# Low weight halves by negated copy and adding DMA in a mixer-and-retrieval block

## The chip, the cores and the metric

The kernel runs on one core of a Trainium2 chip. The metric is device time in microseconds for one execution; a lower time is better. The time before is the median of three runs; beside them one execution was recorded by the hardware profiler, and all durations below are from that one. PE is the matrix engine (TensorE), PEld its weight loads, DVE the VectorE, ACT the ScalarE, POOL the GpSimd, SP the SyncE, which here only issues DMAs.

## The reference

The block has a mixer (norm, modulation, one input projection, a gated short convolution beside a linear recurrence, one output projection) and a retrieval layer with 128 x 128 experts. The second is most of the work:

```python
q = (xb @ w_q).reshape(p, PEER_HEADS, 2, PEER_DK_HALF)
sc = jnp.einsum('phcd,hcnd->phcn', q, sub_keys)
top_s, top_i = lax.top_k(sc, PEER_TOPK)
...
best_s, best_pos = lax.top_k(cand_s, PEER_TOPK)
idx = jnp.take_along_axis(cand_i, best_pos, axis=-1)
g = jax.nn.softmax(best_s, axis=-1)
u_sel = expert_u[idx]
act = jax.nn.gelu(jnp.einsum('phkd,pd->phk', u_sel, xb), approximate=False)
coef = g * act
return jnp.einsum('phk,phkd->pd', coef, expert_v[idx])
```

There are 512 tokens of width 1024, 8 heads, and 16 of 16384 experts for each head and token. All is float32.

## The kernel before, in words

**Dense and sparse.** The 512 tokens are four tiles of 128. For 320 tokens (`NU`) the product with `expert_u` is dense: all 128 blocks of 128 experts ("u chunks") are multiplied on PE and go through Gelu. For the other 192, tile 0 and the first 64 tokens of tile 1 (`XB`), the chosen rows are gathered by indirect DMAs and multiplied on DVE, one row of 128 partitions at a time ("dots", `dots`, line 788): 64 for the part of tile 1 and 128 for tile 0. For tiles 1 to 3 the product with `expert_v` is dense as well ("v chunks"), with coefficients that are the Gelu times a gate matrix. Tile 0 takes 128 gathered sums instead (`sums`, line 804). Dots and sums are 320 steps, each a gather of 512 KB on POOL's queue and one DVE instruction.

**Split weights.** A float32 product is done in three matmuls of a rounded format (`mm3`, lines 92 to 94): high weight by high activation, high by low, low by high. Each weight block of 128 x 1024 is loaded by SP (`load_w`, ring `wraw` of `WR` = 4), rounded by ACT (`high`, line 78, ring `whi` of `WB` = 4), and its low half is the difference, made by DVE (`low`, line 83, ring `wlo` of 4). A buffer of a ring comes free when its last reader is done.

**The order.** After the mixer come the eight query blocks, one a head, and behind each the scores against the keys. The first selections (`stage1` for heads 0 to 3) lie beside them on DVE. Then a hand-written order begins. Iteration `k` of the u loop issues `weights(k)` (the load of block `k + 5`, the low half of block `k + 2`), the matmuls of u chunk `k` with the Gelu of the chunk before, then other work that a planner chooses, and at its end the high half of block `k + 3`. Every engine runs its own queue in the order issued.

**The planner.** It books planned nanoseconds for PE, DVE and ACT (`pe`, `dve`, `ac`), and takes pieces of four generators while `dve` is below `pe`: `s` the selections (top-16, softmax, indices) of tile 1 and then of 2, 3 and 0; `r` the remaining `stage1` pieces; `g` the gate matrices, made from one-hot rows on DVE, ACT and PE and stored to DRAM (`Gd`); `d` the dots. A u chunk books 3530 for PE, 1140 for DVE (the low half) and 1400 for ACT. Dots may start at iteration `first[0]`, four after tile 1's selection is done, and are taken while fewer than `DR * (k + 1 - first[0])` are given, until `CE - QU` = 118. Gates are spread evenly over the chunks from the point where `r` ends. Dots that are left at chunk 124 and all sums are spread evenly over the v chunks. There the gate matrices come back from `Gd`, mostly in reads for 16 chunks at a time (`load_g16`), and some activations from `Ad`.

Of the kernel before, what the change touches and what calls it, by code (L numbers as in the profile page):

```python
# [8 lines left out]
F32 = mybir.dt.float32  # L9
FR = mybir.dt.float32r  # L10
# [3 lines left out]
AF = mybir.ActivationFunctionType  # L14
OP = mybir.AluOpType
# [4 lines left out]
KB = 8  # L20
# [14 lines left out]
def block_kernel(ctx, tc, xT, small, w_ada1, w_ada, b_ada, w_in, w_r, w_i, w_out, w_q, keys, uT, u, v, final_g, out):  # L35
    nc = tc.nc
# [4 lines left out]
    wring = ctx.enter_context(tc.tile_pool(name="wring", bufs=2))  # L41
# [29 lines left out]
    def load_w(src):  # L71
        raw = wring.tile([128, KB, 128], F32, name="wraw", bufs=WR)
        nc.sync.dma_start(raw, src)
        return raw

    def high(raw):
        hi = wring.tile([128, KB, 128], FR, name="whi", bufs=WB)
        nc.scalar.activation(hi, raw, AF.Copy)  # L78
        return hi

    def low(raw, hi):
        lo = wring.tile([128, KB, 128], FR, name="wlo", bufs=WB)
        nc.vector.tensor_sub(lo, raw, hi.bitcast(F32))  # L83
        return lo

    def split_w(raw):
        hi = high(raw)
        return hi, low(raw, hi)

    def mm3(ps, hi, lo, xh, xl, ks, first, last):  # L90
        for k in ks:
            nc.tensor.matmul(ps, hi[:, k, :], xh(k), start=first and k == ks[0], stop=False)  # L92
            nc.tensor.matmul(ps, hi[:, k, :], xl(k), start=False, stop=False)  # L93
            nc.tensor.matmul(ps, lo[:, k, :], xh(k), start=False, stop=last and k == ks[-1])  # L94
# [140 lines left out]
    z_, tn, e_, w_, w2, ac = (l4[:, i, :] for i in range(6))  # L235
# [85 lines left out]
    for cb in range(4):  # L321
# [29 lines left out]
        h = mt("h")  # L351
# [32 lines left out]
    for m in range(KB):  # L384
        if m + 2 < KB:
            oraw[m + 2] = load_w(w_out[m + 2])
        hi, lo = split_w(oraw[m])
# [9 lines left out]
    def x1_mm(i):  # L397
        t, e = divmod(i, 2)
        pt = psZ.tile([128, 4, 128], F32, name="ps_z", bufs=3)
        for k in range(4):  # L400
            nc.tensor.transpose(pt[:, k, :], xs[:, 4 * e + k, t * 128:(t + 1) * 128], ident)
        return i, pt

    def x1_out(i, pt):
        t, e = divmod(i, 2)
        xn = qp.tile([128, T], F32, name="xn")
        nc.scalar.activation(xn, pt, AF.Copy)
        nc.gpsimd.dma_start(x1d[t * 128:(t + 1) * 128, e * 512:(e + 1) * 512], xn)  # L408
# [21 lines left out]
                nc.scalar.activation(dst[:, (k - 3) * 128:(k + 1) * 128], src, AF.Copy)  # L430

    tp_cur = []
    qraw = {0: load_w(w_q[0]), 1: load_w(w_q[1])}
    for k in range(KB):
        t1 = sq_pool.tile([128, T], F32, name="mt1")
        nc.vector.tensor_mul(t1, xs[:, k, :], psr2)
# [35 lines left out]
    qsp = {}  # L472
    early = chain(*(stage1([h], range(NT)) for h in range(HQ)))

    for h in range(8):
        if h + 2 < 8:
            qraw[h + 2] = load_w(w_q[h + 2])
        if h == 0:
            qsp[0] = split_w(qraw[0])
        if h + 1 < 8:  # L480
            qsp[h + 1] = split_w(qraw[h + 1])
        hi, lo = qsp[h]
        ps = psZ.tile([128, T], F32, name="ps_z", bufs=3)
        mm3(ps, hi, lo, lambda k: h2h[:, k, :], lambda k: h2l[:, k, :], range(KB), True, True)
        qT = qp.tile([128, T], F32, name="qT")
        nc.scalar.activation(qT, ps, AF.Copy)
        pss = [psZ.tile([128, NT, 128], F32, name="ps_g", bufs=2) for c in range(2)]
        for t in range(NT):
            for c in range(2):
                nc.tensor.matmul(pss[c][:, t, :], qT[64 * c:64 * c + 64, t * 128:(t + 1) * 128],  # L490
                                 keys_sb[64 * c:64 * c + 64, h, :], start=True, stop=True)
        for _ in range(6 if h >= 2 else 0):
            next(early, None)
        for c in range(2):
            sc[h, c] = scs.tile([128, NT, 128], F32, name="sc", bufs=SCB)
            nc.scalar.activation(sc[h, c], pss[c], AF.Copy)
        if h + 3 < 8:
            x1_out(*x1_mm(h + 3))
# [315 lines left out]
    jobs = [("u", c) for c in range(CE)]  # L814
# [4 lines left out]
    wraw, whi, wlo = {}, {}, {}  # L819
    v0 = max(CE - RB + 3, 0) // 8 * 8 + 8  # L820
    vorder = list(range(v0, NE)) + list(range(v0))
# [7 lines left out]
    def w_high(k):  # L829
        if k < len(jobs):  # L830
            whi[k] = high(wraw[k])

    def w_low(k):
        if k < len(jobs):
            wlo[k] = low(wraw.pop(k), whi[k])

    def weights(k):
        w_load(k + 5)
        w_low(k + 2)
# [4 lines left out]
    def spill(q):  # L844
        nc.sync.dma_start(Ad[q], act[q].rearrange("p c t -> p (c t)"))
        act[q] = None
# [3 lines left out]
    def u_evict():  # L850
        if unread:
            c, ps = unread.pop()
            if c % 2 == 0:
                act[c // 2] = ring.tile([128, 2, NU], F32, name="act", bufs=RB // 2)
            nc.scalar.activation(act[c // 2][:, c % 2], ps, AF.Gelu)  # L855

    def u_chunk(k, pool):
        c = jobs[k][1]
        ps = pool.tile([128, NU], F32, name="ps_act", bufs=2)
        mm3(ps, whi.pop(k), wlo.pop(k), hd, ld, range(KB), True, True)  # L860
        u_evict()
        unread.append((c, ps))
        q = c // 2 - RB // 2 + 2
        if c % 2 == 0 and 0 <= q < v0 // 2:
            spill(q)
        pe[0] += 3530
        dve[0] += 1140
        ac[0] += 1400

    gbuf, g16, gdone = {}, {}, set()  # L870
    coef = {}
# [34 lines left out]
    def v_act(q):  # L906
        if q < NE // 2:
            c = vorder[2 * q] // 2
            if act[c] is None:
                act[c] = ring.tile([128, 2, NU], F32, name="act", bufs=RB // 2)  # L910
                nc.sync.dma_start(act[c].rearrange("p c t -> p (c t)"), Ad[c])
# [24 lines left out]
    pe, dve, ac = [0], [-HEAD], [0]  # L936
# [6 lines left out]
    def turn(k):  # L943

        awake = [g for g in "gsrd" if g in gens and asleep[g] <= k]
        if "d" in awake and (given["d"] >= DR * (k + 1 - first[0]) or k >= CE - QU or xd > k % 2):
            awake.remove("d")
# [16 lines left out]
    for k in range(3):  # L964
        w_high(k)
    for k in range(2):
        w_low(k)
    manual = ExitStack()
    manual.enter_context(tc.manual_schedule())
    for k in range(CE):  # L970
        weights(k)
        u_chunk(k, psE)
        gates_low(4)
        cur[0] = k
# [8 lines left out]
        while dve[0] < RHO * pe[0] or k == KD:  # L983
# [18 lines left out]
            if gopen or g == "d":  # L1002
                given[g] += {"g": 0, "d": 1}.get(g, n)
        w_high(k + 3)
        if k == KD:
            ep.close()
# [47 lines left out]
    for k in range(CE, len(jobs)):  # L1054
        w_load(k + 5)
        w_high(k + 3)
        w_low(k + 2)
        kind, n = jobs[k]
        if kind == "u":
            u_chunk(k, psP)  # L1060
        else:
            q, e = divmod(n, 2)
            v_gates(n + 5)
            if e == 0:
                v_act(q + 4)
                v_gated(q + 1)
            else:
                v_rest(q + 1)
            vsp[n] = [w.pop(k).rearrange("p k e -> p (k e)") for w in (whi, wlo)] + [c[:, e] for c in coef[q]]
            if n < NE - VT:  # L1070
                for b in range(3):
                    v_chunk(n, b)
                del vsp[n]
            u_evict()
            pe[0] += 4090
            dve[0] += 2005
        if kind == "v":
            share = min(max(n + 1 - QV, 0) / (NE - VE - QV), 1) * (steps + 0.31 * (NE - RB)) - 0.31 * max(n + 1 - RB, 0)
            while done < share and next(sparse, None):
                done += 1  # L1080
# [53 lines left out]
XD = 2  # L1134
CE = 124
GB_E = 5
DR = 1.1
QU = 6
QV = 3
RB = 32  # L1140
ZL = 1
XE = 5
WB = 4
# [51 lines left out]
```

## Time and profile before

| | us |
|---|---|
| median of 3 runs | 1411.64 |
| lowest, highest | 1409.84, 1411.95 |
| the profiled execution | 1413.22 |
| its span | 1411.5 |

| stretch of the span, us | what runs |
|---|---|
| 0 to 255 | modulation, mixer, output projection, second norm |
| 255.0 to 309.3 | eight query blocks and scores |
| 309.3 to 403.7 | u chunks 0 to 23 |
| 403.7 to 832.1 | u chunks 24 to 123 |
| 832.1 to 863.2 | v chunks 0 to 3, u chunks 124 to 127 between them |
| 863.2 to 1382.8 | v chunks 4 to 124 |
| 1382.8 to 1411.5 | the last three v chunks, last additions, final norm |

The share of busy time on the page is an average over these stretches, and each has its own limit; busy time by stretch and the waits within one say more. Matmuls are pipelined: a PE that is busy all the time is at its peak only if the count of matmuls in the stretch is also at its highest. In the groups of instructions the columns are line, engine, operation, output from inputs, shapes, count, then busy time and mean nanoseconds, then the engine's idle time just before with what ended it.

### The profile page before, as it was taken

The page shows a single profiled execution, that of the slowest core. Times are in us where ns is not written, and L with a number is a line of the kernel's source. Part 1 is how long each engine was busy: PE and PEld are TensorE (multiplying, and loading weights), DVE is VectorE, ACT ScalarE, POOL GpSimd, SP SyncE. Part 2 cuts the span into 40 slices and gives each one's busy share as a digit, 9 for nine tenths or more (in the row PEclk, how much of TensorE's full clock was granted, in tenths as well). Part 3 has the DMA queues.
Part 4 walks back from the last instruction along what each step waited for, and adds up shares of the span by engine and source line. Part 5 has one row for each costly group of instructions (what it writes and reads, how often), then busy time and mean ns, then how long its engine had stood idle before and what let it go on. Part 6 is the DMA issues. An engine that isn't in the chain of part 4 may idle for free.

```text
span 1411.5 us, 21746 instructions
## 1 busy us (share of the span) xinstructions
PE 1336.9 (95%) x7739; PEld 1144.7 (81%) x7739; DVE 1222.1 (87%) x2332; ACT 687.6 (49%) x1178; POOL 538.0 (38%) x334
## 2 busy tenths in 40 slices
PE   5999998999998999999999999899989999999995
PEld 2666787779998999998989998777778888878884
DVE  6766555899998999999989847799989889898998
ACT  4544433545377697797744444233333434343442
POOL 0000000000233145344545404576666667576760
PEclk9999999999999999999999999999999999999998
DMA  9675322124678899999999997999999999999994
GB/s 378 225 265 181 124 90 97 61 83 134 203 253 300 290 344 397 357 355 355 417 382 388 403 314 244 411 378 410 403 415 411 404 404 416 412 405 410 406 382 165
DMA packets 146929, 440.07 MB, mean 312 GB/s; under 512 B 14722, under 2 KB 42370, under 8 KB 144772
## 3 DMA queue, kind: packets, MB, share of 16 engines
q1 hardware_dynamic: 99812, 267.75, 51.5%
q0 software_dynamic: 46720, 169.89, 30.8%
q8 instruction: 60, 0.98, 0.3%
q10 hardware_dynamic: 288, 1.05, 0.2%
q14 instruction: 49, 0.40, 0.1%
HBM read 393.54 MB, written 45.09 MB: 311 GB/s over the span
## 4 chain that ended last, share of the span: by engine, by line
DVE 27%; PE 23%; DMA 16%; issue 13%; ACT 4%; DVEq 0%; SPq 0%; ACTq 0%
DMA wraw<-in_v_dram 13%; DVE wlo L83 5%; PE ps_act L92 5%; PE ps_act L94 5%; PE ps_act L93 5%; PE acc L1037 5%; DVE scr L788 4%; DVE ys L804 4%; DMA Gd<-stg 2%; DVE cf L920 2%; DVE cl L931 2%; DVE oh L627 2%; ACT whi L78 1%; DVE rep L457 1%; PE ps_gt L658 1%
## 5 line engine op out<-in xcount | busy, mean ns | idle before, releaser
L78 ACT ACTIVATE whi<-wraw 128x1024 fp32r<-128x1024 f32 x292 | 308.7, 1057 | 404.1 <-DMA wraw<-in_v_dram 157.7
L83 DVE TENSOR_TENSOR wlo<-wraw,whi 128x1024 fp32r<-128x1024 f32 x292 | 356.1, 1220 | 112.5 <-ACT whi L78 111.3
L92 PE MATMUL ps_act<-h,whi 128*128 128x320 f32 x1024 | 322.5, 315 | 8.1 <-ACT act L855 6.9
L94 PE MATMUL ps_act<-h,wlo 128*128 128x320 f32 x1024 | 317.1, 310 | 0.6 <-DVE wlo L83 0.6
L93 PE MATMUL ps_act<-h,whi 128*128 128x320 f32 x1024 | 317.1, 310 | 0.0
L767 POOL DMA_INDIRECT rows<-in_u_dram,idx_s x128 | 201.3, 1573 | 189.0 <-DVE scr L788 162.4
L767 POOL DMA_INDIRECT rows<-in_v_dram,idx_s x128 | 222.7, 1740 | 108.7 <-DVE ys L804 84.9
L1037 PE MATMUL acc<-whi,ch 128*128 128x512 f32 x750 | 233.7, 393 | 9.5 <-ACT ch L924 9.2
L1037 PE MATMUL acc<-whi,cl 128*128 128x512 f32 x750 | 234.6, 394 | 6.1 <-DVE cl L931 6.1
L1037 PE MATMUL acc<-wlo,ch 128*128 128x512 f32 x750 | 233.6, 393 | 0.0
L767 POOL DMA_INDIRECT rows<-in_u_dram,idx_b x64 | 108.9, 1701 | 255.7 <-DVE scr L788 171.8
L92 PEld LDWEIGHTS ps_act<-h,whi 128*128 128x128 f32 x1024 | 193.2, 189 | 10.8 <-ACT act L855 8.7
L94 PEld LDWEIGHTS ps_act<-h,wlo 128*128 128x128 f32 x1024 | 192.9, 188 | 0.9 <-DVE wlo L83 0.9
L93 PEld LDWEIGHTS ps_act<-h,whi 128*128 128x128 f32 x1024 | 193.3, 189 | 0.2
L1037 PEld LDWEIGHTS acc<-whi,ch 128*128 128x128 f32 x750 | 141.6, 189 | 40.7 <-ACT ch L924 10.9
L1037 PEld LDWEIGHTS acc<-whi,cl 128*128 128x128 f32 x750 | 141.6, 190 | 40.1 <-DVE cl L931 11.1
L1037 PEld LDWEIGHTS acc<-wlo,ch 128*128 128x128 f32 x750 | 142.1, 189 | 29.9
L804 DVE SCALAR_TENSOR_TENSOR ys<-rows,acts,ys 128x1024 f32<-128x1024 f32 x127 | 162.6, 1281 | 1.7
L788 DVE SCALAR_TENSOR_TENSOR scr<-rows,h2n 128x1024 f16<-128x1024 f32 x128 | 156.2, 1220 | 2.3 <-DMA rows<-in_u_dram,idx_s 0.6
L643 ACT ACTIVATE igh<-oh,gl 128x128 f16<-128x128 f16 x320 | 104.0, 432 | 47.8 <-DVE oh L627 47.6
L408 POOL DMA_DIRECT2D x1d<-xn x8 | 4.6, 569 | 281.7 <-DVE wlo L83 234.6
L92 PE MATMUL ps_z<-h,whi 128*128 128x512 f32 x224 | 90.8, 409 | 3.2 <-ACT h L216 2.9
(260 smaller groups left out, 1691.2 us busy)
## 6 DMA issues: line engine op xcount, KB each, us to landing
wraw<-in_uT_dram SPq DMA_DIRECT2D x128, 512.0 KB, 6.8
wraw<-in_v_dram SPq DMA_DIRECT2D x128, 512.0 KB, 9.3
Gd<-stg SPq DMA_DIRECT2D x46, 512.0 KB, 9.2
wada<-in_w_ada_dram SPq DMA_DIRECT2D x16, 1024.0 KB, 5.1
Ad<-act SPq DMA_DIRECT2D x48, 320.0 KB, 7.1
act<-Ad SPq DMA_DIRECT2D x48, 320.0 KB, 12.2
h<-Gd SPq DMA_DIRECT2D x12, 1024.0 KB, 18.3
wraw<-in_w_in_dram SPq DMA_DIRECT2D x20, 512.0 KB, 6.1
```

Of the source, the lines that this page charges most:

```text
L78: nc.scalar.activation(hi, raw, AF.Copy)
L83: nc.vector.tensor_sub(lo, raw, hi.bitcast(F32))
L92: nc.tensor.matmul(ps, hi[:, k, :], xh(k), start=first and k == ks[0], stop=False)
L93: nc.tensor.matmul(ps, hi[:, k, :], xl(k), start=False, stop=False)
L94: nc.tensor.matmul(ps, lo[:, k, :], xh(k), start=False, stop=last and k == ks[-1])
L627: nc.vector.tensor_tensor(flat.rearrange("p (q n b) -> p q n b", q=8, b=2), io2[:, None, :, :].to_broadcast(shp), sij[:, a0].rearrange("p ...
L643: nc.scalar.activation(ig[:, 1, k // 2, :, k % 2], of[:, k // 2, 0, :, k % 2], AF.Copy, scale=gl[:, t0 + k:t0 + k + 1])
L767: nc.gpsimd.indirect_dma_start(out=r[:, :], out_offset=None, in_=table, in_offset=bass.IndirectOffsetOnAxis(ap=idxs[:, k:k + 1], axis=0))
L788: nc.vector.scalar_tensor_tensor(scr, rows.pop(n), 1.0, hn, op0=OP.mult, op1=OP.mult, accum_out=dst[:, k:k + 1])
L804: nc.vector.scalar_tensor_tensor(ys, rows.pop(k), acts[:, k:k + 1], ys, op0=OP.mult, op1=OP.add)
L920: nc.vector.tensor_mul(cf[:, :, XB:].rearrange("p c (g t) -> p c g t", t=16), act.pop(vorder[2 * q] // 2).rearrange("p c (g t) -> p c g t" ...
L1037: nc.tensor.matmul(accs[b][e], st[:, bs], mv[:, e * 512:(e + 1) * 512], start=first, stop=last)
```

## The change

The low half is raw minus high. The new helper forms it in another order: ACT writes the negated high half into the low buffer, and a DMA that adds to its destination brings the raw block from DRAM onto it. That DMA is issued from POOL's queue. The helper is used for u blocks 3 to 23 (21 of them) and query blocks 2 to 7 (six). The ACT copy and the POOL DMA of block `k + 3` stand at the end of iteration `k`, where only the high half stood; the DVE subtraction of these blocks, which stood at the start of iteration `k + 1`, is gone. The raw block is still loaded by SP for the high half, so it is read from DRAM twice. Query blocks are loaded one head earlier, and their high half is formed two heads ahead, not one. The planner books nothing on DVE for these low halves and 2350 instead of 1400 on ACT. `DR` goes from 1.1 to 1.2.

```diff
+    def low_dma(src, hi):
+        lo = wring.tile([128, KB, 128], FR, name="wlo", bufs=WB)
+        nc.scalar.activation(lo, hi.bitcast(F32), AF.Copy, scale=-1.0)
+        nc.gpsimd.dma_start(lo, src, accum_op=OP.add)
+        return lo
...
-    qraw = {0: load_w(w_q[0]), 1: load_w(w_q[1])}
+    qraw = {h: load_w(w_q[h]) for h in range(3)}
...
-        if h + 2 < 8:
-            qraw[h + 2] = load_w(w_q[h + 2])
+        if h + 3 < 8:
+            qraw[h + 3] = load_w(w_q[h + 3])
         if h == 0:
             qsp[0] = split_w(qraw[0])
-        if h + 1 < 8:
-            qsp[h + 1] = split_w(qraw[h + 1])
+            qsp[1] = split_w(qraw[1])
+        if h + 2 < 8:
+            whq = high(qraw[h + 2])
+            qsp[h + 2] = whq, low_dma(w_q[h + 2], whq)
...
     def w_high(k):
         if k < len(jobs):
             whi[k] = high(wraw[k])
+            if 3 <= k < LN:
+                del wraw[k]
+                wlo[k] = low_dma(uT[jobs[k][1]], whi[k])
 
     def w_low(k):
-        if k < len(jobs):
+        if k < len(jobs) and k not in wlo:
             wlo[k] = low(wraw.pop(k), whi[k])
...
-        dve[0] += 1140
-        ac[0] += 1400
+        dve[0] += 0 if 3 <= k + 2 < LN else 1140
+        ac[0] += 2350 if 3 <= k + 3 < LN else 1400
...
-DR = 1.1
+DR = 1.2
...
+LN = 24
```

## The prediction

> **What bounds the kernel now.** I read the page's busy shares first, then its chain that ended last, then busy time stage by stage, then the waits inside the stages.
>
> ```profile
> PE 1336.9 (95%) x7739; PEld 1144.7 (81%) x7739; DVE 1222.1 (87%) x2332; ACT 687.6 (49%) x1178; POOL 538.0 (38%) x334
> DVE 27%; PE 23%; DMA 16%; issue 13%; ACT 4%; DVEq 0%; SPq 0%; ACTq 0%
> ```
>
> PE looks full, but the chain changes hands between DVE, PE and DMA, so what an edit is worth has to be read stage by stage. The stage table has, for each stretch, its length, then busy time and count of PE, PEld, DVE, ACT and POOL, then clock, DMA share and GB/s.
>
> ```profile
> 255.00:309.30 54.30, 51.68 (x321) 40.57 (x319) 49.23 (x285) 23.92 (x39) 2.16 (x4) 1.00 0.25 78
> 309.30:403.70 94.40, 88.84 (x611) 86.80 (x612) 93.64 (x403) 46.29 (x78) 14.08 (x9) 1.00 0.51 167
> 403.70:700.30 296.60, 285.46 (x2257) 279.33 (x2255) 287.74 (x554) 237.34 (x529) 122.79 (x73) 0.99 0.94 346
> 700.30:832.10 131.80, 127.17 (x894) 126.30 (x892) 107.86 (x188) 56.43 (x93) 53.17 (x36) 0.99 1.02 385
> 863.20:1382.80 519.60, 504.29 (x2180) 411.99 (x2179) 480.46 (x524) 192.16 (x246) 340.09 (x201) 0.99 1.02 401
> 1382.80:1411.50 28.70, 12.71 (x55) 9.87 (x53) 24.23 (x58) 7.44 (x21) 0.00 (x0) 0.81 0.28 106
> 793.43:828.63 35.20, 35.20 (x242) 35.20 (x241) 20.52 (x24) 15.12 (x22) 9.14 (x7) 1.00 1.04 386
> 1252.03:1292.83 40.80, 40.80 (x182) 33.80 (x180) 40.59 (x38) 15.86 (x20) 30.57 (x17) 1.00 1.03 404
> ```
>
> The last two rows are undisturbed stretches: ten u chunks in 35.2 us, so 3.52 us for the 24 matmuls of one, and ten v chunks in 40.8 us, so 4.08 us. (The count includes a matmul cut off at each end.) They are PE's floor.
>
> The first 24 u chunks fill 309.3 to 403.7. Their floor is 24 x 3.52 = 84.5, plus 32 gate matmuls for which the planner books 1.8: 86.3. They take 94.4, so 8.1 us is lost there. DVE is busy for 93.64 of the 94.4: it is the bound, while DMA stands at half.
>
> The whole u stage, 309.3 to 832.1, takes 522.8 against 124 x 3.52 = 436.5 plus about 51 of gate matmuls by the planner's own costs (40 steps at 920 ns, 16 at 890 ns): 35 us lost, 27 of them after chunk 23. The v stretch 863.2 to 1382.8 holds 121 chunks: 519.6 against 121 x 4.08 = 493.7, so 25.9 us lost, with DMA at 1.02 and DVE at 480 of 520 busy. It has little slack on three resources at once. Where it loses:
>
> ```profile
> 899.90:923.40 23.50, 18.57 (x73) 14.50 (x73) 15.94 (x24) 7.97 (x12) 10.68 (x7) 0.93 0.99 383
> 1026.90:1046.40 19.50, 15.59 (x55) 12.02 (x54) 16.53 (x22) 7.38 (x9) 10.07 (x6) 0.82 1.04 413
> 1230.50:1248.00 17.50, 14.52 (x56) 11.16 (x55) 15.52 (x15) 7.38 (x9) 8.90 (x6) 0.90 1.04 414
> ACT whi L78 <- DMA wraw<-in_v_dram: 157.7, 52, 9.6
> PEld acc L1037 <- DVE cl L931: 11.1, 13, 2.5
> PEld acc L1037 <- ACT ch L924: 10.9, 4, 4.7
> ```
>
> The three stretches hold 4 chunks (16.3 us) in 23.5, and 3 chunks (12.2) in 19.5 and in 17.5: 19.8 of the 25.9. In the waits (total, times, longest), ACT sits at a high half whose block has not landed, so the coefficients behind it in ACT's queue are late for PE; a smaller part is DVE.
>
> **The change part by part.** The sum starts from the profiled execution, 1413.2 us (span 1411.5 and 1.7 around it); the median shown is 1.6 lower.
>
> (a) Six query blocks. DVE loses six subtractions, ACT gains six copies, POOL six DMAs.
>
> ```profile
> L78 ACT ACTIVATE whi<-wraw 128x1024 fp32r<-128x1024 f32 x292 | 308.7, 1057 | 404.1 <-DMA wraw<-in_v_dram 157.7
> L83 DVE TENSOR_TENSOR wlo<-wraw,whi 128x1024 fp32r<-128x1024 f32 x292 | 356.1, 1220 | 112.5 <-ACT whi L78 111.3
> x1d<-xn POOLq DMA_DIRECT2D x8, 256.0 KB, 3.3
> ```
>
> DVE saves 6 x 1.22 = 7.3. ACT pays 6 x 1.06 = 6.4 in a stage where it works 23.9 of 54.3. A head takes 54.3/8 = 6.8, and the adding DMA is issued two heads ahead: some 11 us after the two copies, against 3.3 for half such a transfer. PE sets the pace there, so **0**. If that cover went, PE would wait for the rest of the landing. What remains is that DVE reaches chunk 0 with up to 7 us less behind it.
>
> (b) Chunks 3 to 23. DVE loses 21 x 1.22 = 25.6 and ACT gains 21 x 1.06 = 22.3 (its 46.3 of 94.4 becomes 69). But the planner books zero for these on DVE, so it pulls other DVE work forward until each chunk's budget is full again. The chunks do not become lighter; the work behind them does. What changes in place is the wait. PE needed a DVE subtraction; now it needs ACT, ACT again, POOL and a DMA.
>
> ```profile
> 320.16 0.44 ACT L855 ACTIVATE act<-ps_act 128x320 f32<-128x320 f32 x1 [2.14 <-PE ps_act L94]
> 320.49 1.05 ACT L78 ACTIVATE whi<-wraw 128x1024 fp32r<-128x1024 f32 x1
> wraw<-in_uT_dram SPq DMA_DIRECT2D x22, 512.0 KB, 3.6
> rows<-in_u_dram,idx_b POOLq DMA_INDIRECT x9, 5.9
> L767 POOL DMA_INDIRECT rows<-in_u_dram,idx_b x64: 933/1682/2077, 365.0 to 650.4; - x64
> DMA to landing us min/median/max: 5.2/8.4/10.3
> ```
>
> In this undisturbed spot chunk 3 has just begun (ACT evicts chunk 2 at 320.16) and the high half of chunk 6 ends at 321.54, some 1.6 us into the chunk. The negated copy adds 1.06 and hand-over 0.1: issue at 2.8 us, need at 3 x 3.52 = 10.56. So **the adding DMA has 7.8 us** from issue to landing. The trace has no adding DMA. The nearest rows, over this stage: a plain load of 512 KB lands in 3.6, a POOL gather of the same bytes in 5.9 (8.4 over all 64 of its kind, under load). Below, a plain landing of 3.6; above, everything twice, 11.8 here and 17 under load. I take the gather, nearest in queue and size, plus one more pass for reading the destination (0.524 MB at 410 GB/s, 1.3): 7.2. That just fits. From about chunk 14 on, gathers stand ahead of it in POOL's queue, which waits there for DVE to free a row buffer; there I take 8.4 + 1.3 = 9.7, late by 1.9. A high buffer is free only when the chunk four before is done, so lateness is paid once per four chunks: 2.5 turns, 5 us. Of the old 8.1 lost I keep 5 (transposes and gates still wait for DVE). Together **+2**; ends -6 (nothing is late and DVE is ahead) and +25 (below). Queued behind a late issue on POOL are the gathers, and so DVE's dots; on ACT nothing waits for the DMA, but each eviction stands behind one more copy.
>
> The Trainium skill, "DMA: Bandwidth & Descriptors", section "Anatomy of one DMA — SWDGE (gpsimd) path", gives 2.0 us plus bytes/436e3 for a POOL-issued DMA: 3.2 us here, an estimate by which nothing would be late. The gathers' 5.9 disagrees. "SBUF — State Buffer", section "Who interferes with whom", speaks against the change: GpSimd cannot write descriptors while certain DVE operations hold a shared port. The issues of 0.93 to 2.08 us in the row agree in kind with such a block; by their spread alone a DMA would be 1.1 us later, some 6 us over five turns of the buffers.
>
> (c) Chunks 24 to 123. By the planner's sums, tile 1's selection is done one iteration earlier, so `first` is 16, not 17. Dots are taken until iteration 117 while fewer than DR x (k + 1 - first): 1.1 x 101 = 111.1, so 112 dots before the v stage, against 1.2 x 102 = 122.4, so 123.
>
> ```profile
> 309.30:832.10 522.80, 137.45 (x224) 0.99 0.88 324
> 419.80:429.50 9.70, 6.47 (x57) 5.88 (x57) 9.53 (x23) 5.70 (x17) 2.19 (x2) 0.91 1.02 364
> 468.50:476.30 7.80, 6.37 (x58) 5.49 (x57) 7.70 (x25) 3.98 (x12) 0.95 (x2) 1.00 0.98 366
> 648.90:658.60 9.70, 6.42 (x56) 5.91 (x56) 9.63 (x14) 6.69 (x20) 6.13 (x5) 0.89 0.95 306
> ```
>
> The first row is the dots' own line: 224 instructions, two a dot, 112 as the sum has it. The others are chunks 28, 39 and 82, where the planner places two wide gate steps together: 27.2 us for 3 x (3.52 + 1.84) = 16.1, 11 us lost. Walked through with the change, the planner does so once (chunk 70), so some 7 come back. Against it, eleven more dots load a DMA already at 0.94 to 1.02, and the gate stores share it; I allow 3. **-4**, ends -11 (all three go, the stores lose nothing) and +6 (none goes, twice the allowance).
>
> (d) The v stage has 320 - 123 = 197 dots and sums instead of 208.
>
> ```profile
> DMA packets 75565, 208.51 MB, mean 401 GB/s; under 512 B 6300, under 2 KB 27804, under 8 KB 75532
> L804 DVE SCALAR_TENSOR_TENSOR ys<-rows,acts,ys 128x1024 f32<-128x1024 f32 x127 | 162.6, 1281 | 1.7
> L788 DVE SCALAR_TENSOR_TENSOR scr<-rows,h2n 128x1024 f16<-128x1024 f32 x128 | 156.2, 1220 | 2.3 <-DMA rows<-in_u_dram,idx_s 0.6
> ```
>
> Eleven gathers are 5.8 MB of 208.5: 14 us at 401 GB/s. On DVE they are 11 x 1.30 = 14 us too. PE can give back at most its 25.9. Three-quarters of that (the 19.8) falls into bursts: by the code the three stretches are those in which gate blocks are read for chunks 16, 48 and 96 on, and such a read holds SP's queue for long:
>
> ```profile
> h<-Gd SPq DMA_DIRECT2D x12, 1024.0 KB, 18.3
> ```
>
> Lighter traffic shortens the bursts but need not remove them. I take **-10**, ends 0 and -14. The tail does not change.
>
> Sum: 0 + 2 - 4 - 10 = -12: 1401.2 for a profiled execution, **1400 us** as a median.
>
> **The rivals.**
> 1. Slower: the adding DMA is late at every turn of the four weight buffers. It decides from about 12 us issue to landing: (12 - 7.8) x 5.25 turns = 22, less the 8 that overlap what DVE already loses, is the 14 gained elsewhere. At the upper ends, 11.8 for ten chunks and 17 for the rest: 2.5 x 4.0 + 2.5 x 9.2 = 33, less 8: +25, minus 14: +11, about 1423. For it: reading the destination can double the traffic, and POOL's queue is shared. Against: DMA stands at 0.51 in this stage. The port block that "SBUF — State Buffer" of the Trainium skill describes would be a share of this rival, not all of it.
> 2. Nothing comes back in v: the bursts come from the gate blocks, not from gathers. v -2, chunks 24 to 123 at -1 because the added dots crowd the stores, early +2: -1, about 1411. For it: each of the three large stalls is such a burst. Against: DMA is over 1.0 in between as well.
> 3. All of it: nothing late (-2 in the early chunks), -7 and -14: 23 less, about 1389.
>
> **How the numbers follow.** Forecast 0.50 (its own range 1391 to 1408), rival 1 0.17, rival 2 0.20, rival 3 0.13. A measurement of this kernel tells some 0.2%, 2.8 us, from no change. Faster: 0.50 + 0.13 + half of rival 2 = 0.74 (0.11 of it from rival 2); within 0.2%: 0.09; slower: 0.17. The range takes in rival 3 and the lower part of rival 1: 1386 to 1420.
>
> **What would show it.** Right: adding DMAs that land in 6 to 10 us; 123 dots before the v stage; the first 24 chunks within 92 to 102 us; double gate stretches gone; v chunks 4 to 124 in about 510 us, with about 203 MB. Wrong: PE waiting for `wlo` from a DMA by more than 14 us in total, a v stretch that still takes 519, or chunks 24 to 123 longer than 428.

## The result and the profile after

| | before | after |
|---|---|---|
| median, us | 1411.03 (8 runs) | 1421.24 (8 runs) |
| lowest, highest | 1408.99, 1412.03 | 1417.28, 1428.09 |
| the profiled execution | 1413.22 | 1420.64 |
| its span | 1411.5 | 1418.9 |

The ratio is 1.0074, with a 95% interval of 1.0055 to 1.0093: slower, where the forecast was faster. The time lies just above the range and close to the 1423 of rival 1.

The page of the kernel after: busy time by engine, then the engines' shares of the chain that ended last.

```profile
PE 1342.0 (95%) x7739; PEld 1150.4 (81%) x7739; DVE 1192.8 (84%) x2305; ACT 714.5 (50%) x1205; POOL 547.2 (39%) x361
PE 40%; DVE 21%; DMA 17%; issue 16%; ACT 5%; POOL 2%; DVEq 0%; SPq 0%; POOLq 0%; ACTq 0%
```

DVE has lost 27 instructions and 29 us, as intended, and is a smaller part of the chain. The time is longer all the same. The stage table of the kernel after says where (length; busy time and count of PE, PEld, DVE, ACT, POOL; clock, DMA share, GB/s):

```profile
255.00:310.50 55.50, 52.40 (x323) 41.12 (x322) 45.47 (x282) 29.15 (x45) 6.60 (x9) 0.99 0.50 126
310.50:430.60 120.10, 99.88 (x647) 96.96 (x648) 98.92 (x476) 81.28 (x127) 34.00 (x33) 0.92 0.92 246
430.60:855.90 425.30, 411.58 (x3110) 404.06 (x3110) 381.00 (x670) 279.80 (x591) 173.06 (x115) 0.99 0.97 367
887.00:1392.70 505.70, 499.22 (x2179) 408.74 (x2179) 469.06 (x504) 191.60 (x246) 325.96 (x190) 1.00 1.02 402
```

| stretch | before | after | difference | forecast |
|---|---|---|---|---|
| start to u chunk 0 | 309.3 | 310.5 | +1.2 | 0 |
| u chunks 0 to 23 | 94.4 | 120.1 | +25.7 | +2 |
| u chunks 24 to 123 | 428.4 | 425.3 | -3.1 | -4 |
| v chunks 0 to 3 with u chunks 124 to 127 | 31.1 | 31.1 | 0 | |
| v chunks 4 to 124 | 519.6 | 505.7 | -13.9 | -10 |
| tail | 28.7 | 26.2 | -2.5 | 0 |
| sum | 1411.5 | 1418.9 | +7.4 | -12 |

Everything that the change was to bring has come; one stretch of 24 chunks takes more than all of it. The weight-load count there is 648 against 612 (some cut off at the ends among them): the planner, with DVE booked lighter, places 64 gate matmuls in it instead of 32, so its floor rises by 1.8, from 86.3 to 88.1. The time lost over the floor goes from 8.1 to 32.0. The stretch in two parts, chunks 0 to 13 and 14 to 23, in the kernel after:

```profile
310.50:369.60 59.10, 54.95 (x340) 54.03 (x341) 58.40 (x350) 39.18 (x52) 12.38 (x13) 0.92 0.90 212
369.60:430.60 61.00, 44.92 (x310) 42.94 (x309) 40.52 (x128) 42.10 (x76) 21.62 (x20) 0.92 0.93 278
```

Before, the two took 55.9 and 38.5. In the first DVE is still busy all the time, and 3.2 us are lost; the other 22.5 are lost in the second, where neither PE nor DVE is. PE's waits for the adding DMAs in this stretch (total, times, longest), once as its weight loads see them and once as its matmuls do:

```profile
PEld ps_act L100 <- DMA wlo<-in_uT_dram: 21.4, 8, 5.8
PE ps_act L100 <- DMA wlo<-in_uT_dram: 19.4, 8, 5.6
```

Some 20 us in eight waits, at the third matmul of a chunk (L100, the first that reads the low half), for the adding DMA. The rest is mostly the clock. Four short windows in the same form; the granted clock is the third number from the end:

```profile
310.20:317.00 6.80, 6.51 (x25) 6.51 (x26) 6.80 (x48) 0.24 (x1) 0.02 (x1) 0.52 0.71 157
381.90:388.70 6.80, 5.47 (x21) 5.47 (x22) 4.42 (x8) 0.29 (x1) 0.86 (x1) 0.52 1.05 246
347.00:350.40 3.40, 3.40 (x15) 3.40 (x15) 3.37 (x13) 0.11 (x1) 0.86 (x1) 0.56 1.03 286
412.00:415.40 3.40, 3.40 (x15) 3.40 (x15) 3.15 (x8) 0.00 (x0) 2.79 (x3) 0.54 1.06 290
```

In 3.4 us PE does 15 matmuls there instead of some 23 (24 in 3.52). Busy time by the missing share of the clock, 3.1 + 2.6 + 1.5 + 1.6, makes 8.8 us. The first window is at chunk 0, behind the scores; in each of the other three, or just ahead of it, a wait of PE for the adding DMA ends (5.56 us long at 383.23, 1.90 at 346.79, 4.53 at 411.56). A wait of 2.84 that ends at 372.89 has no such window. So 19.4 + 8.8 = 28.2 of the 32.0 have a name, though the 3.1 at chunk 0 need not come from the change (last section). The Trainium skill, "TensorE: Matmul & The Clock Gate", section "What's actually happening", states windows of about 3.4 us and half clock behind an idle one; the lengths of 3.4 and 6.8 agree. The wait of 1.90 is shorter than such a window and has a half-clock stretch behind it all the same.

### The profile page after: what moved, and what is told of

The parts are those of the page before. It is cut to its first block, busy times and chain, and to the rows that moved or that the text cites. A ratio compares the mean times of both kernels' runs of the same rounds, so it can differ in the third digit from the quotient of the medians.

```text
span 1418.9 us, 21796 instructions
## 1 busy us (share of the span) xinstructions
PE 1342.0 (95%) x7739; PEld 1150.4 (81%) x7739; DVE 1192.8 (84%) x2305; ACT 714.5 (50%) x1205; POOL 547.2 (39%) x361
## 4 chain that ended last, share of the span: by engine, by line
PE 40%; DVE 21%; DMA 17%; issue 16%; ACT 5%; POOL 2%; DVEq 0%; SPq 0%; POOLq 0%; ACTq 0%
DMA wraw<-in_v_dram 12%; PE ps_act L98 6%; PE ps_act L100 5%; PE ps_act L99 5%; PE ps_z L98 5%; PE ps_z L100 5%; PE ps_z L99 5%; DVE wlo L83 3%; DVE ys L812 3%; DVE scr L796 3%; DVE cl L942 2%; DVE cf L931 2%; DMA wlo<-in_uT_dram 2%; PE acc L1048 2%; PE ps_gt L666 2%
## 5 line engine op out<-in xcount | busy, mean ns | idle before, releaser
L83 DVE TENSOR_TENSOR wlo<-wraw,whi 128x1024 fp32r<-128x1024 f32 x265 | 323.6, 1221 | 120.3 <-ACT whi L78 119.2
L100 PE MATMUL ps_act<-h,wlo 128*128 128x320 f32 x1024 | 322.4, 315 | 19.4 <-DMA wlo<-in_uT_dram 19.4
L98 PE MATMUL ps_act<-h,whi 128*128 128x320 f32 x1024 | 326.7, 319 | 3.5 <-ACT act L866 2.4
L99 PE MATMUL ps_act<-h,whi 128*128 128x320 f32 x1024 | 321.3, 314 | 0.0
L775 POOL DMA_INDIRECT rows<-in_u_dram,idx_s x128 | 194.5, 1519 | 229.1 <-DVE scr L796 176.0
L775 POOL DMA_INDIRECT rows<-in_v_dram,idx_s x128 | 226.5, 1770 | 116.9 <-DVE ys L812 96.1
L100 PEld LDWEIGHTS ps_act<-h,wlo 128*128 128x128 f32 x1024 | 196.8, 192 | 21.6 <-DMA wlo<-in_uT_dram 21.4
L98 PEld LDWEIGHTS ps_act<-h,whi 128*128 128x128 f32 x1024 | 197.2, 193 | 5.1 <-ACT act L866 3.1
L99 PEld LDWEIGHTS ps_act<-h,whi 128*128 128x128 f32 x1024 | 197.4, 193 | 0.2
L775 POOL DMA_INDIRECT rows<-in_u_dram,idx_b x64 | 96.9, 1514 | 118.9 <-DVE scr L796 103.8
L866 ACT ACTIVATE act<-ps_act 128x320 f32<-128x320 f32 x128 | 55.2, 431 | 103.2 <-PE ps_act L100 101.4
L89 POOL DMA_DIRECT2D wlo<-in_w_q_dram x6 | 5.5, 916 | 247.8 <-ACT wlo L88 247.4
```

Of the source, the lines that this page charges most:

```text
L775: nc.gpsimd.indirect_dma_start(out=r[:, :], out_offset=None, in_=table, in_offset=bass.IndirectOffsetOnAxis(ap=idxs[:, k:k + 1], axis=0))
```

## Why the adding DMA lands late: three candidates

The trace after shows three, and the experiments were to tell them apart.

**Slow packets.** The first adding DMA of the u stage (q0) runs beside 0.77 MB of other traffic (q1) in its 10 us. The DMA view of these 10 us of the kernel after (queue: packets, MB, share of 16 engines), then the issue with KB and us to landing:

```profile
q0 software_dynamic: 144, 0.52, 34.2%
q1 hardware_dynamic: 221, 0.77, 20.5%
...
wlo<-in_uT_dram POOLq DMA_DIRECT2D x1, 512.0 KB, 7.4
```

34.2% of 10 us is 3.4 us of all 16 engines for 0.52 MB. Over the whole stretch of the kernel after:

```profile
q0 software_dynamic: 4634, 16.90, 62.7%
...
wraw<-in_uT_dram SPq DMA_DIRECT2D x22, 512.0 KB, 7.8
wlo<-in_uT_dram POOLq DMA_DIRECT2D x20, 512.0 KB, 9.7
```

The DMA share there is 0.92 at only 246 GB/s; the v stretch needs 402 GB/s to reach 1.02. The engines are full without moving much, and the plain loads on SP land in 7.8 where they took 3.6.

**Gathers ahead.** ACT's negated copy for chunk 15 in the kernel after (start, us, instruction), POOL's timeline around it (with the idle time before and what ended it), then PE's at that chunk:

```profile
365.70 1.06 ACT L88 ACTIVATE wlo<-whi 128x1024 fp32r<-128x1024 f32 x1
```

```profile
364.69 0.86 POOL L89 DMA_DIRECT2D wlo<-in_uT_dram  x1 [5.67 <-ACT wlo L88]
366.17 1.05 POOL L775 DMA_INDIRECT rows<-in_u_dram,idx_b  x1 [0.61 <-issue]
367.52 1.83 POOL L775 DMA_INDIRECT rows<-in_u_dram,idx_b  x1 [0.30 <-issue]
369.66 1.04 POOL L775 DMA_INDIRECT rows<-in_u_dram,idx_b  x1 [0.30 <-issue]
371.00 0.94 POOL L775 DMA_INDIRECT rows<-in_u_dram,idx_b  x1 [0.30 <-issue]
371.94 1.95 POOL L89 DMA_DIRECT2D wlo<-in_uT_dram  x2
```

```profile
383.23 0.64 PE L100 MATMUL ps_act<-h,wlo 128*128 128x320 f32 x1 [5.56 <-DMA wlo<-in_uT_dram]
```

POOL's first row is the DMA of chunk 14; that of chunk 15 is the first of the two in the last row. Its copy ended at 366.76, but POOL issues four gathers of 512 KB first and comes to it at 371.94, 5.2 us later. Then the data of the gathers go first as well: the fourth lands 9.2 us after its issue, at 380.2, and the block at 383.2, 11.2 us after its own. So gathers ahead cost twice, in POOL's time and in the DMA queue. The Trainium skill, "DMA: Bandwidth & Descriptors", section "Two DMAs through the same engine are not ordered", says that descriptors of one queue on one engine start in order; the order of these landings agrees with it.

**Late issue.** ACT's timeline of the kernel after, where it makes the negated copy for chunk 14:

```profile
361.97 0.28 ACT L613 ACTIVATE selB<-ps_t 128x128 f32<-128x128 f32 x1 [2.12 <-DVE gl L610]
...
362.25 1.06 ACT L78 ACTIVATE whi<-wraw 128x1024 fp32r<-128x1024 f32 x1
363.34 1.06 ACT L88 ACTIVATE wlo<-whi 128x1024 fp32r<-128x1024 f32 x1
```

The pieces that the planner adds to a chunk stand ahead of the copies in ACT's queue. Here one of them waits for DVE, the copy ends at 364.40, and the DMA is issued at 364.69 (POOL's first row above). Its chunk begins at 369.60 and reads the low half for the first time at 372.89, late by 3.0 though the DMA takes 8.2, hardly more than the 7.8 us of lead forecast; some 5 of these are left. It is not this chunk alone. Of the eight late blocks seven (4, 7, 8, 14, 15, 19 and 20) were issued only 4.9 to 6.4 us before their chunk began; the other fourteen blocks were all issued 7.9 us or more before it, and of them only 21 was late, by 1.0.

## The experiments

Each ratio is to the kernel before, run beside it. All but one start from the kernel after.

**Fewer blocks: 11 instead of 21, none once gathers begin.**

```diff
-LN = 24
+LN = 14
```

> The adding DMAs are kept for the queries and u blocks 3 to 13, and dropped for 14 to 23 (LN 14); DR stays 1.2. By the planner's sums 123 dots still lie before the v stage. In the changed kernel the first 24 u chunks take 120.1 us (94.4 before), and PE waits 21.4 us for adding DMAs: some 4.6 in chunks 4 to 8 and some 16 in chunks 14 to 21. Theory A (queue): the cost arises where adding DMAs stand behind row gathers in POOL's queue; then the first 24 chunks fall to 96 to 104 us, the v stretch stays near 506, and the total is 1398 to 1405. Theory B (rate): an adding DMA moves its bytes at half the rate of a plain one (328 against 159 ns a packet of 4 KB) and each one costs alike; then half of the loss stays, the first 24 chunks take about 108 and the total is about 1409. Theory C (late issue: ACT gets to the copies late because it waits for DVE first): also about half, 1409.

1399.72 us, ratio 0.9915 (0.9900 to 0.9929): faster than both. Its first 24 chunks, then 24 to 123, then v 4 to 124, then its wait:

```profile
310.20:408.90 98.70, 94.12 (x659) 92.10 (x660) 97.67 (x458) 66.50 (x119) 26.51 (x23) 0.97 0.85 243
408.90:833.20 424.30, 410.17 (x3099) 402.33 (x3097) 390.01 (x695) 283.65 (x590) 180.02 (x115) 0.99 0.97 366
866.70:1371.90 505.20, 498.75 (x2180) 409.99 (x2180) 469.07 (x504) 191.56 (x246) 319.42 (x190) 0.99 1.02 402
```

```profile
PEld ps_act L100 <- DMA wlo<-in_uT_dram: 5.8, 5, 1.9
```

Blocks 14 to 23 cost 21.4 of stretch (120.1 - 98.7) and bring nothing: 123 dots and the same v stretch without them. The numbers are those of the theory that gathers ahead in POOL's queue are the cause, but this edit also takes away the late issues and half of the slow packets.

**The same DMA without the addition.**

```diff
-        nc.gpsimd.dma_start(lo, src, accum_op=OP.add)
+        nc.gpsimd.dma_start(lo, src)
```

> All 27 adding DMAs become plain POOL DMAs of the same block to the same place, after the same ACT copy: the low half is then the raw block, so the low part of these products is not computed. Theory B (rate): the packets fall from 328 to about 160 ns, waits of PE for these DMAs fall from 21 to under 5 us, the first 24 chunks to about 100, the total to about 1401. Theory A (queue): behind four gathers a plain DMA is late too, so waits in chunks 14 to 21 stay at 8 us or more and the total is 1408 to 1414. Theory C (late issue): hardly a change, 1418 or more.

1416.71 us, ratio 1.0036 (1.0023 to 1.0050). The stretch, its wait, and the first such DMA of the u stage with what ran beside it in 10 us:

```profile
311.10:425.90 114.80, 97.36 (x646) 94.99 (x647) 98.66 (x475) 81.11 (x127) 26.47 (x33) 0.93 0.77 267
```

```profile
PEld ps_act L100 <- DMA wlo<-in_uT_dram: 12.7, 4, 4.4
```

```profile
q1 hardware_dynamic: 341, 1.26, 34.6%
q0 software_dynamic: 144, 0.52, 15.7%
```

The same 144 packets take 15.7% instead of 34.2%: adding makes a packet 2.2 times as long here, though more ran beside the plain DMA. That explains some 9 us of the wait (21.4 to 12.7), and all of it at chunk 4; the waits at chunks 14, 15 and 20 stay (3.2, 4.4 and 4.2 us). It is a cause, not the only one. The stretch gains only 5.3, because PE's weight loads now wait 6.6 us for ACT's evictions, where it was 1.1. The total fits none of the three theories.

**Dots at the old rate.**

```diff
-DR = 1.2
+DR = 1.1
```

> The change with DR left at 1.1: by the planner's sums 113 dots before the v stage instead of 123. If the v stage gains by the eleven steps that leave it (13.7 us by the two profiles), it goes back to about 518 us and the total is 1430 to 1435, the first 24 chunks staying near 120. If the v stage's gain has another cause, the total stays at 1421. If the denser dots are what makes the early chunks late, those fall to about 110 instead.

1425.71 us, ratio 1.0103 (1.0088 to 1.0119): 113 dots; the first 24 chunks, then v 4 to 124:

```profile
309.70:428.80 119.10, 97.30 (x647) 93.77 (x648) 98.96 (x476) 81.17 (x127) 34.22 (x33) 0.94 0.92 247
880.70:1396.90 516.20, 502.92 (x2180) 409.47 (x2179) 481.19 (x525) 191.92 (x246) 340.75 (x200) 0.99 1.02 404
```

The early loss doesn't come from the rate of dots. The total came out below the expectation, because chunks 24 to 123 take 420.8, 4.5 less than with 123 dots.

**No gathers before iteration 20.**

```diff
-        if sready and not first:
+        if sready and not first and k >= 20:
```

> The change with all 21 adding DMAs, but the first gathers are issued at iteration 20 or later, so no gather stands ahead of an adding DMA in POOL's queue up to block 22. The dots start at chunk 24, so only some 113 lie before the v stage, which goes back to about 518 us. Theory A (queue): waits of PE for adding DMAs in chunks 14 to 21 fall from 16 to under 4 us, the first 24 chunks take 96 to 104; total 1410 to 1417. Theory B (rate) and theory C (late issue): waits stay at 15 us or more in all, the first 24 chunks at 112 or more; total 1425 or more.

1423.06 us, ratio 1.0088 (1.0070 to 1.0105). The stretch and its wait:

```profile
309.70:428.10 118.40, 100.09 (x646) 97.18 (x647) 93.68 (x483) 81.05 (x127) 23.02 (x25) 0.91 0.88 231
```

```profile
PEld ps_act L100 <- DMA wlo<-in_uT_dram: 15.9, 7, 4.0
```

With the queue free of gathers until chunk 20, chunk 14 is still late by 4.0 us. The theory that the gathers alone do it falls. Block 14's DMA is issued at 363.85 here, some 5 us before the block is needed, as in the kernel after.

**Copies and DMA issued first.** The high half, the negated copy and the DMA move from the end of the iteration to just behind the chunk's matmuls.

```diff
         u_chunk(k, psE)
+        if k + 3 < LN:
+            w_high(k + 3)
...
-        w_high(k + 3)
+        if k + 3 >= LN:
+            w_high(k + 3)
```

> All 21 adding DMAs; in iterations 0 to 20 the high half, its negated copy and the adding DMA of block k + 3 are issued right behind the matmuls of chunk k, ahead of what the planner adds, instead of behind it. So far the 20.6 us that PE waits for adding DMAs in the first 24 chunks fell only to 15.2 without gathers ahead of them and to 12.3 with plain DMAs in their place, and chunk 14's was issued 4 to 5 us before its chunk in all three. Theory C (late issue: ACT reaches the two copies late, behind planner's work that waits for DVE): the issue comes within 3 us of the start of chunk k for nearly all, waits fall under 9 us, the first 24 chunks to 98 to 106, total 1400 to 1408. Theory D (the landing alone, 8 to 15 us, is longer than the 7.8 us there are, whenever it is issued): waits stay at 15 us or more and the total at 1417 or more.

1412.11 us, ratio 1.0004 (0.9993 to 1.0016). Its stretch, its wait, and POOL's timeline:

```profile
309.80:423.30 113.50, 96.69 (x647) 93.88 (x648) 99.16 (x477) 81.33 (x127) 34.26 (x33) 0.92 0.97 263
```

```profile
PEld ps_act L100 <- DMA wlo<-in_uT_dram: 18.3, 7, 6.0
```

```profile
365.58 1.05 POOL L775 DMA_INDIRECT rows<-in_u_dram,idx_b  x1 [0.30 <-DVE rep L463]
...
371.34 1.95 POOL L89 DMA_DIRECT2D wlo<-in_uT_dram  x2
```

Chunks 14 and 15 are no longer late; now 16 (6.0 us) and 21 (5.3), whose DMAs stand behind gathers, are: block 16's copy ends at 367.19, and POOL comes to its DMA at 371.34. The edit doesn't take all late issues away: block 8's DMA is issued at 335.27, 4.9 us before its chunk begins, and PE's weight load waits 4.1 us for it. So late issue behind the planner's pieces is not the only cause either: where it is taken away, another takes its place, though the stretch is 6.6 us shorter.

**Both: early issue and no gathers before iteration 20** (the last two edits together).

> Both edits together on the change: the copies and the adding DMA right behind the chunk's matmuls (e5), and no gather before iteration 20 (e4). Alone they left 17.2 and 15.2 us of PE's 20.6 us of waits for adding DMAs. Theory E (several covers: a block is late by the issue or by the gathers, and taking one away leaves the other): together the waits fall under 8 us, most of it at chunks 4 and 8, the first 24 chunks to 98 to 105; about 113 dots, so the v stretch near 515 and a total of 1405 to 1411. Theory D (the landing alone is too long): waits of 12 us or more, total 1416 or more.

1409.45 us, ratio 0.9985 (0.9972 to 0.9999). The stretch and its wait:

```profile
309.70:414.60 104.90, 93.72 (x646) 90.39 (x647) 89.33 (x468) 81.02 (x127) 23.17 (x25) 0.98 0.93 238
```

```profile
PEld ps_act L100 <- DMA wlo<-in_uT_dram: 9.1, 7, 3.4
```

Both go together: the wait is less than half, the clock is back at 0.98, and the stretch is the shortest of those with 21 blocks. Of what is left 3.4 us is at chunk 8, whose DMA is issued 4.9 us before its chunk begins here too. With 113 dots the v stage stays long, so the time isn't that of 11 blocks.

**Early issue and no addition** (the second edit and that of the copies issued first).

> The early issue of e5 with plain DMAs in place of adding ones (the low part of these products is not computed); the gathers stay. Alone the two left 17.2 and 12.3 us of waits. Theory E: with the landing halved and the issue early there is room even behind four gathers: waits under 5 us, the first 24 chunks at 96 to 102, total 1396 to 1403. If the gathers ahead in the queue are enough by themselves, chunks 16 and 21 still wait 3 us each or more and the total is 1405 or more.

1408.33 us, ratio 0.9971 (0.9955 to 0.9987); the stretch takes 108.0, and the wait is

```profile
PEld ps_act L100 <- DMA wlo<-in_uT_dram: 9.7, 4, 3.9
```

Chunks 16 and 21, behind gathers, still wait 3.0 and 3.9 us with plain packets: gathers ahead are enough by themselves. At chunk 16 that is POOL's time as well as the queue: its copy ends at 366.89, its issue comes at 371.76. The weight loads' waits of these six kernels side by side:

| wait for the low half, us | copies at the end of the iteration | copies first |
|---|---|---|
| as in the change | 21.4 | 18.3 |
| no gathers before 20 | 15.9 | 9.1 |
| no addition | 12.7 | 9.7 |

One remedy takes away 3 to 9 us, two take 12. The causes overlap: where one is taken away, the next is often enough to make the same chunk late. All three remedies together, and no gathers with no addition, were not tried.

**The low half used last.** For chunks 0 to 23 the matmuls with the low weights come behind the other sixteen, so the DMA has two thirds of a chunk more, 2.3 us.

```diff
-        mm3(ps, whi.pop(k), wlo.pop(k), hd, ld, range(KB), True, True)
+        if k < LN:
+            hi, lo = whi.pop(k), wlo.pop(k)
+            for j in range(KB):
+                nc.tensor.matmul(ps, hi[:, j, :], hd(j), start=j == 0, stop=False)
+                nc.tensor.matmul(ps, hi[:, j, :], ld(j), start=False, stop=False)
+            for j in range(KB):
+                nc.tensor.matmul(ps, lo[:, j, :], hd(j), start=False, stop=j == KB - 1)
+        else:
+            mm3(ps, whi.pop(k), wlo.pop(k), hd, ld, range(KB), True, True)
```

> All 21 adding DMAs, issued where the change issues them; in chunks 0 to 23 the 8 matmuls that use the low half come last, behind the 16 that use the high half, so PE needs the low half 2.3 us later into the chunk. If lateness is a matter of each block by itself, every wait is cut by 2.3: 1.8, 0.8, 2.1, 3.0, 5.7, 1.4, 4.7, 1.2 become 0, 0, 0, 0.7, 3.4, 0, 2.4, 0, some 6.5 us; with less of the halved clock behind them the first 24 chunks fall from 120 to about 102 and the total to 1400 to 1407. If the weight buffers hold it (a later end of the chunk delays the block four later by as much), waits stay at 12 us or more and the total at 1413 or more.

1414.98 us, ratio 1.0022 (1.0005 to 1.0039). Two waits of its first 24 chunks:

```profile
PEld ps_act L877 <- DMA wlo<-in_uT_dram: 13.8, 7, 4.6
PEld ps_act L874 <- ACT act L866: 6.1, 3, 4.1
```

By the expectation's sum some 14 of the wait should go (a wait shorter than 2.3 saves only its length); 7.6 do, and the waits for ACT's evictions grow by 5.0, from 1.1. The numbers are those that were expected if the weight buffers hold it, but the trace shows another cause. PE waits at chunks 6 and 13 for an ACT that itself waits for DVE, 3.0 and 5.3 us:

```profile
327.76 1.91 ACT L577 ACTIVATE oh<-pf 128x2048 f16<-128x2048 f16 x1 [3.04 <-DVE pf L566]
361.25 0.28 ACT L613 ACTIVATE selB<-ps_t 128x128 f32<-128x128 f32 x1 [5.32 <-DVE gl L610]
```

DVE is busy for 53.4 of the 54.1 us from chunk 0 to 364.0, as it was for nearly all of this stage in the kernel before. What PE no longer waits for the DMAs there it waits for DVE, by way of ACT.

**The parts that should cost nothing or stand alone.** The six query blocks alone, and the new rate of dots alone, in the kernel before (the second with `DR = 1.2` there):

```diff
-DR = 1.2
+DR = 1.1
...
-LN = 24
+LN = 0
```

> Only the six query blocks have adding DMAs (LN 0), DR 1.1. The prediction gave this part nothing: total within 1408 to 1414, u chunk 0 starting within 1 us of 309.3, and the first 24 chunks shorter than 94.4 by 1 to 5 us, since DVE comes to them with up to 7 us less behind it. If the adding DMAs are late for the queries too, u chunk 0 starts at 312 or later.

> The kernel before with DR 1.2 and nothing else. By the planner's sums 115 dots lie before the v stage instead of 112, since DVE has no room for more: the total is 1405 to 1411, the v stretch 514 to 519. If DR alone were what shortens the v stage, 123 dots would show and the stretch would be near 506.

The query blocks alone: 1411.95 us, ratio 1.0002 (0.9989 to 1.0015); chunks 0 to 23 take 94.50. The rate alone: 1409.28 us, ratio 0.9986 (0.9973 to 0.9998), with 115 dots. Their v stretches, one row each:

```profile
867.30:1385.20 517.90, 502.79 (x2180) 410.51 (x2179) 481.28 (x525) 191.77 (x246) 353.37 (x201) 0.99 1.02 403
```

```profile
865.90:1380.30 514.40, 500.30 (x2180) 408.77 (x2180) 476.99 (x519) 191.60 (x246) 344.73 (x198) 0.99 1.02 403
```

The rate by itself hardly moves dots, because DVE's bookings are full; the freed DVE of chunks 3 to 13 is what makes room for 123.

**Fewer blocks and the low half last** (the first edit and the one of chunks 0 to 23, here 0 to 13).

> Adding DMAs for blocks 3 to 13 alone (e1) and the low matmuls last in chunks 0 to 13 (e6). In e1 PE still waits 1.4, 1.7 and 1.8 us in chunks 4, 7 and 8. With the need 2.3 us later all three vanish: first 24 chunks at 94 to 96 instead of 98.7, total 1394 to 1398 beside 1399.7. Rival: DVE's lag takes over as it did in e6 (a PE wait for ACT of 4.0 us at chunk 5), and the total stays at 1398 to 1401.

1396.18 us, ratio 0.9889 (0.9868 to 0.9910). The wait falls from 5.8 to

```profile
PEld ps_act L877 <- DMA wlo<-in_uT_dram: 3.1, 5, 1.5
```

but the stretch stays at 98.6, where 94 to 96 were expected, and the span of both profiled executions is 1398.0. Its interval overlaps that of the 11 blocks alone, so the two are not told apart; both beat the kernel before by some 1%. A deeper ring of weight buffers, which would give more lead, was not tried.

## The prediction against the runs, step by step

- **(a) Query blocks: 0.** Right for the time: alone they make a ratio of 1.0002. In that run u chunk 0 starts at 310.9, 1.6 us later than before, where 1 was allowed; over all profiles it starts at 309.7 to 311.1 with these blocks, and at 309.3 and 309.9 in the two without. DVE's head start at chunk 0 brings nothing either (94.50 against 94.40).
- **(b) Chunks 3 to 23: +2. This step failed: +25.7.** The term that was mis-sized is the lateness, 5 us (2.5 turns of 1.9): PE waits 19.4 us for the adding DMAs, and the half clock takes 8.8 more, 5.7 of it behind these waits. The chain was right (ACT, ACT, POOL, DMA). "Lateness is paid once per four chunks" held in part: the late ones come in groups, at chunks 4, 7 and 8, at 14 and 15, at 19 to 21, but neighbours both pay (2.8 us at 14, 5.6 at 15). Four things in it were wrong:
  - "7.2. That just fits." The first of the u stage lands in 6.6 to 7.6 us over six profiles, so the figure was good for one. But 21 of them fill the DMA engines: the share goes from 0.51 to 0.92, and the median landing is 9.7, which no longer fits into 7.8. In the 10 us above the addition takes 1.9 us more of all 16 engines (34.2% against 15.7%), where one more pass was put at 1.3. "DMA stands at 0.51 in this stage", the argument against rival 1, was read from the kernel without these DMAs.
  - "From about chunk 14 on 9.7." From issue to landing it is 11.2 at chunk 15 and 13.6 to 15.3 at chunks 16, 17 and 21 to 23. POOL did not wait for a free row buffer at chunk 15: it spent 5.2 us on issuing four gathers between that chunk's copy and its DMA, and then their data went first.
  - "Issue at 2.8 us into the chunk." That was read from one undisturbed chunk. Where a planned piece on ACT waits for DVE, the copy stands behind it (chunk 14); seven of the eight late blocks had 4.9 to 6.4 us until their chunk began instead of 7.8.
  - A wait was priced at its length. The half clock behind three of them costs 5.7 us more; no term had that.
  - The Trainium skill's 3.2 us for a POOL-issued DMA of this size ("DMA: Bandwidth & Descriptors", "Anatomy of one DMA — SWDGE (gpsimd) path") is not what one with an addition takes, 6.6 to 7.6 for the first of the stage. The port block of the Trainium skill's "SBUF — State Buffer" was no large part: POOL's issues of the adding DMA last 0.85 to 1.35 us (the tile's view of the kernel after: shortest, median, longest in ns, first and last start):

```profile
L89 POOL DMA_DIRECT2D wlo<-in_uT_dram x21: 854/863/1352, 309.4 to 410.3; - x21
```

- **(c) Chunks 24 to 123: -4.** Measured -3.1; 123 dots, as worked out. That the sum is so close is in part luck. In the three kernels with 21 blocks and 113 dots these chunks take 418.8 to 420.8, in the five with 123 dots 425.3 to 427.9: ten more dots cost some 7 there, where 3 was allowed. The other part is then some -9 against 428.4, where -7 was forecast, and 1.8 of it are the 32 gate matmuls that moved to the first 24 chunks. Whether the double gate steps make up the rest was not taken apart.
- **(d) The v stage: -10.** The mechanism is right, the size a little small: -13.9, nearly the end of its range, -14, the whole of eleven steps. The bytes are those forecast:

```profile
DMA packets 74106, 203.17 MB, mean 402 GB/s; under 512 B 6145, under 2 KB 27649, under 8 KB 74073
```

  Over the kernels, 112 or 113 dots give 513.9 to 519.6 and 123 dots 503 to 507: some 1.1 us a step. So the bursts did shrink, against rival 2: of the three large stalls that the prediction lists, those at v chunks 41 and 42 and at 89 and 90 are gone but for 1.4 us at chunk 43, and that at 13 and 14 stays, with 5.1 us. A step that leaves the v stage saves 1.1 there and, by (c), costs some 0.7 before it. The tail gave 2.5 more, for which there was no term.
- **The rivals.** Rival 1, the adding DMA late, is what happened, at nearly its price (1421.24 against 1423). That its number came so close is in part luck: it had landings of 11.8 and 17, at every turn, where the median is 9.7 and eight blocks of 21 are late; late issue and the clock, which it did not have, make up the rest. The forecast named PE waiting for `wlo` by over 14 us as the sign against it; it is some 20. Of rivals 2 and 3, the v part of the third came true.

## What to carry to other kernels

Work that is taken from a busy engine is worth what that engine can pull forward with it, and no more: here 11 blocks made room for all the dots that the rate allows, and the other ten only cost. An adding DMA has to be priced in DMA engine time and in its place in the queue, and its lead counted from the latest moment at which the copy ahead of it can stand in its engine's order and the issuing engine comes to it, not from a quiet chunk. A stall of the matrix engine is priced with the half clock that may follow it: here it did behind three waits (5.56, 1.90 and 4.53 us), and not behind one of 2.84.

## What the runs showed of the hardware

- In 10 us with one such DMA, a DMA that adds took 2.2 times the engine time of the same 144 packets without the addition (34.2% against 15.7%). The first of the u stage, 512 KB, landed in 6.6 to 7.6 us over six profiles. Plain loads beside 21 of them land in 7.8 us (median) instead of 3.6; with the addition left out, in 5.3.
- A transfer on POOL's queue behind four gathers of 512 KB was issued 5.2 us after its copy was done, since POOL issued the gathers first, and landed 11.2 us after that.
- The half-clock window at chunk 0 (310.2) has no counterpart in the kernel before, where the clock is 1.00 through chunks 0 to 23. Just before it PE waits 1.2 us for the scores on ACT, in all thirteen profiles alike. Of the eleven with adding DMAs for the query blocks five have a half-clock window there, 3.4 or 6.8 us long, and six have none, nor have the two without. The run with dots at the old rate is one of the six, and its first 24 chunks still take 119.1 us against 120.1. What tips the clock there was not settled.
